# Strassen output projection: product 3 accumulates onto product 5's PSUM bank, with another product order

## Chip, cores and metric

The kernel runs on one core of one Trainium2 chip. The metric is the device time of one execution in microseconds (us); lower is better. The engines named below are TensorE (PE in the profile; its weight loads are PEld), VectorE (DVE), ScalarE (ACT), GpSimd (POOL) and SyncE (SP), whose instruction stream here only issues DMA transfers.

## What is computed

One layer of a decoder trunk. Four head groups (a convolution module, causal pooling, stick-breaking attention, cross-attention into memory) make a mixed activation of 2048 columns for 2048 prompt tokens and for 32 sample tokens; that is projected to 1024 columns, normalised twice and added to the residual. The change touches only the projection and what follows it:

```python
mix = jnp.concatenate([y_c * silu(cg), y_p * silu(pg), y_s * silu(sg), y_m * silu(mg)], axis=-1)
out = rms_norm(mix @ w_out, post_g)      # 2048 x 2048 @ 2048 x 1024
...
y_prompt = rms_norm(x + out, final_g)
```

Everything is float32.

## The kernel before

The product `mix @ w_out` is done by the Strassen-Winograd scheme: tokens are split in two row blocks (even and odd tiles of 128 tokens), the inner dimension in two halves, the output columns in two halves of 512, and seven products of half-size blocks replace eight. The products carry the numbers 1, 7, 2, 6, 4, 5, 3. Product `prod` for token block `i` (0 to 7, each a pair of token tiles 2i and 2i+1) is called (prod, i) here; block 8 (`LAST`, L1545) holds the 32 sample tokens and takes only products 1, 2, 5 and 3.

`order` (L1883 to L1887) lists the products as TensorE runs them; TensorE's order is written by hand, the order on the other engines is made by the program's planner when it is built, from the order in which the code emits the instructions and from estimated durations. `parts` splits each product into two halves h of the inner dimension. The loop at L2051 walks over the parts. For each one `out_part` (L1922) issues the matmuls: 4 chunks of 128 inner rows, each with three matmuls (high times high, high times low, low times high, since each float32 factor is split in a rounded high part and a low remainder), so 24 matmuls of 128x512 for a whole product, all summed in one PSUM bank (`acc`). There are eight banks in rotation by then (`accp`, `accp2`). Ahead of the matmuls, `prepare` (L2035) loads the rows (`out_load`, DMA on SP), adds or subtracts row blocks (`out_combine`, POOL or DVE), rounds to the high part (`out_high`, ACT) and `lows` has DVE make the low part (`out_low`, L1696, tile `ml`), some two products ahead. The right-hand factors are prepared in the same way (`weight_sum`, `weight_high`, `weight_low`, L1586 to L1597).

When a product is complete, `out_ready` (L1702) takes it out. `U2` and `U3` are sums of products 1, 7 and 6, one SBUF tile of 128x512 for each token block.

* Product 4: DVE adds U3 in place in PSUM (L1740), ACT sums its squares (`square`, L1700), DVE multiplies by `post_g` (L1743). This is the left half of token tile 2i+1.
* Product 5: DVE first adds the product to U2 (L1739), then adds U3 to the product in place in PSUM (L1740); squares and the multiplication follow. This is the right half of tile 2i+1, which is now whole, and `out_tile` ends it.
* Product 3: DVE adds U2 (which by now contains product 5) in place; squares and multiplication follow. This is the right half of tile 2i, and `out_tile` ends that one. Its left half, `c11`, was put to DRAM earlier; `out_first` (L1752) fetches it into one of two buffers (`oh`) and `out_factor` (L1758, POOL) multiplies it by `post_g`.

`out_tile` (L1761) loads the residual rows `xt` (tile `oxt`), turns the sums of squares into a factor (L1769 on DVE, L1770 on ACT, L1771 on DVE), adds the residual half by half (L1775, DVE), sums squares again (L1776, ACT), makes the second factor (L1779, L1780, L1781), scales the tile (L1786, DVE) and stores it (L1788). The closing part of tile 15 is put off and emitted within that of tile 14, the last tile of the program.

Of the kernel before, what the change touches and what calls it, by code (L numbers as in the profile page):

```python
# [13 lines left out]
ALU = mybir.AluOpType  # L14
# [73 lines left out]
def kernel(  # L88
# [9 lines left out]
    pe, act, dve, pool, sp = nc.tensor, nc.scalar, nc.vector, nc.gpsimd, nc.sync  # L98
# [1446 lines left out]
    LAST = 8  # L1545
# [152 lines left out]
    def square(c, t, half):  # L1698
        rows = P if t < 16 else NS
        act.activation(out=junk[:rows], in_=c[:rows], func=AF.Square, accum_out=ssk[:rows, t, half : half + 1])  # L1700

    def out_ready(prod, i, o):  # L1702

        if i == LAST:
            if prod == 5:
                return
            both = (ope.tile([P, 512], F32, tag="oh", name="both3", bufs=OH) if prod == 3 else
                    op.tile([P, 512], F32, name=f"both{prod}", bufs=1))
            act.copy(both[:NS], o[NS : 2 * NS])
            dve.tensor_tensor(out=both[:NS], in0=both[:NS], in1=o[:NS], op=ALU.add)  # L1710
            if prod == 1:
                keep["s"] = both
            elif prod == 2:
                dve.tensor_tensor(out=both[:NS], in0=both[:NS], in1=keep["s"][:NS], op=ALU.add)
                square(both, 16, 0)
                keep[16, 0] = both
            else:
                dve.tensor_tensor(out=o[:NS], in0=both[:NS], in1=keep["s"][:NS], op=ALU.add)
                square(o, 16, 1)
                dve.tensor_tensor(out=o[:NS], in0=o[:NS], in1=gpost[:NS, 512:], op=ALU.mult)  # L1720
                dve.tensor_tensor(out=keep[16, 0][:NS], in0=keep[16, 0][:NS], in1=gpost[:NS, :512], op=ALU.mult)
                out_tile(16, keep[16, 0], o)
            return
        t = 2 * i + (prod in (4, 5))
        if prod == 1:
            act.copy(U2[:, i], o)
        elif prod == 7:
            dve.tensor_tensor(out=U3[:, i], in0=o, in1=U2[:, i], op=ALU.add)
        elif prod == 6:
            dve.tensor_tensor(out=U3[:, i], in0=o, in1=U3[:, i], op=ALU.add)  # L1730
            dve.tensor_tensor(out=U2[:, i], in0=o, in1=U2[:, i], op=ALU.add)
        elif prod == 2:
            c = opw.tile([P, 512], F32, tag="c11", name=f"c11_{i}", bufs=1)
            dve.tensor_tensor(out=c, in0=o, in1=U2[:, i], op=ALU.add)
            square(c, t, 0)
            sp.dma_start(c11d[i], c)
        else:
            if prod == 5:
                dve.tensor_tensor(out=U2[:, i], in0=o, in1=U2[:, i], op=ALU.add)  # L1739
            dve.tensor_tensor(out=o, in0=o, in1=(U2 if prod == 3 else U3)[:, i], op=ALU.add)  # L1740
            half = 0 if prod == 4 else 1
            square(o, t, half)
            dve.tensor_tensor(out=o, in0=o, in1=gpost[:, 512 * half : 512 * half + 512], op=ALU.mult)  # L1743
            keep[t, half] = o
            if prod != 4:
                out_tile(t, keep[t, 0], keep[t, 1])
            if (prod, i) == (3, 0):
                out_first(2)
            if prod == 5 and i != 2 or (prod, i) == (3, 1):
                out_factor(2 if prod == 3 else i)  # L1750
# [10 lines left out]
    def out_tile(t, a, b):  # L1761

        rows = P if t < 16 else NS
        xt = ope.tile([P, D], F32, tag="oxt", name=f"oxt{t}", bufs=OX)[:rows]
        sp.dma_start(xt, xp[P * t : P * t + P, :] if t < 16 else xs)
        if t != 14:
            keep["ss"] = ope.tile([P, 6], F32, tag="oss", name=f"oss{t}", bufs=1)
        ss = keep["ss"][:rows, 3:] if t == 14 else keep["ss"][:rows]
        dve.tensor_tensor(out=ss[:, 0:1], in0=ssk[:rows, t, 0:1], in1=ssk[:rows, t, 1:2], op=ALU.add)  # L1769
        act.activation(out=ss[:, 0:1], in_=ss[:, 0:1], func=AF.Sqrt, bias=eps_t[:rows], scale=1.0 / D)  # L1770
        dve.reciprocal(out=ss[:, 0:1], in_=ss[:, 0:1])  # L1771
        last = t == 14
        halves = (slice(0, 512), slice(512, 1024))
        for n, (hs, src) in enumerate(zip(halves, (a[:rows], b[:rows]))):
            dve.scalar_tensor_tensor(out=xt[:, hs], in0=src, scalar=ss[:, 0:1], in1=xt[:, hs], op0=ALU.mult, op1=ALU.add)  # L1775
            act.activation(out=junk[:rows], in_=xt[:, hs], func=AF.Square, accum_out=ss[:, n + 1 : n + 2])  # L1776
        if last:
            keep.pop("end")()
        dve.tensor_tensor(out=ss[:, 1:2], in0=ss[:, 1:2], in1=ss[:, 2:3], op=ALU.add)  # L1779
        act.activation(out=ss[:, 1:2], in_=ss[:, 1:2], func=AF.Sqrt, bias=eps_t[:rows], scale=1.0 / D)  # L1780
        dve.reciprocal(out=ss[:, 1:2], in_=ss[:, 1:2])  # L1781
        dst = y_prompt[0, P * t : P * t + P, :] if t < 16 else y_sample.rearrange("b t d -> (b t) d")

        def end():
            for n, hs in enumerate(halves if last else (slice(0, 1024),)):
                dve.scalar_tensor_tensor(out=xt[:, hs], in0=xt[:, hs], scalar=ss[:, 1:2], in1=gfin[:rows, hs],  # L1786
                                         op0=ALU.mult, op1=ALU.mult)
                (wq if n else sp).dma_start(dst[:, hs], xt[:, hs])  # L1788

        if t == 15:  # L1790
            keep["end"] = end
        else:
            end()
# [90 lines left out]
    order += [(p, i) for i in range(2, 6) for p in (2, 6)] + [(2, 6), (2, 7), (2, 8), (6, 6), (6, 7)]  # L1884
    last_ = len(order)
    order += [(4, 0), (4, 1), (5, 0), (5, 1), (4, 2), (5, 2), (3, 0), (3, 1), (3, 2), (5, 8), (3, 8)]
    order += [(p, i) for i in range(3, 8) for p in (4, 5, 3)]  # L1887
    parts = [(p, i, h) for p, i in order for h in range(2)]
    last_ *= 2
    lead_ = parts[: 2 * LEAD]  # L1890
    raws, mix, accs, keep, stores = {}, {}, {}, {}, []
# [30 lines left out]
    def out_part(x):  # L1922

        prod, i, h = x
        rows = P if i < LAST else 2 * NS
        cont = i == LAST and prod == 3
        bank = 5 if cont else prod, i
        if bank not in accs:
            p_ = accp if accp2 is None or len(accs) % 8 < 3 else accp2
            accs[bank] = p_.tile([P, 512], F32, tag="acc", name=f"acc{prod}_{i}", bufs=3 if p_ is accp else 5)  # L1930
        o, m = accs[bank], mix.pop(x)
        for k in range(4):

            ms = ((0, 0), (0, 1), (1, 0)) if i < LAST else ((0, 0), (0, 1))
            for n, (a, w) in enumerate(ms):
                pe.matmul(o[:rows], lhsT=m[a][:, k, :rows], rhs=W[prod, 4 * h + k][w],  # L1936
                          start=not cont and h == k == n == 0,
                          stop=h == 1 and k == 3 and n == len(ms) - 1 and (prod != 5 or i < LAST))
            yield
        if h:  # L1940
            done.append((prod, i, o))
# [109 lines left out]
    for n, x in enumerate(parts):  # L2051
        if n == last_:
            ow.close()
            x6.close()
            ope = oy.enter_context(tc.tile_pool(name="ope", bufs=1, side="right", reuse_waits="tile"))
            gpost = ope.tile([P, D], F32, name="gpost", bufs=1)
            gfin = ope.tile([P, D], F32, name="gfin", bufs=1)
            sp.dma_start(gpost, post_g[0].partition_broadcast(P))
            sp.dma_start(gfin, final_g.partition_broadcast(P))
        prod, i, h = x  # L2060
        if prod == 4 and not h and i != 2:
            out_first(i)
        while (prod, 4 * h + 3) not in W:
            weights_step(wait)
        lows(n + 1)
        for k, p_ in enumerate(out_part(x) if n >= len(lead_) else lead if not n else ()):
            conv_due += 1.0
            while conv_due >= (OPACE if ("conv", 0) in flags else OPACE0):
                conv_due -= OPACE if ("conv", 0) in flags else OPACE0
                next(conv, None)  # L2070
            weights_step(n + k % 4 / 4)
            if not n:

                k, at_ = p_ % 4, p_ // 4
            else:
                at_ = n
            if k % 4 == LOWK:
                lows(at_ - 1 + AHEAD)
            if not n and k == 3:
                prepare(at_ + AHEAD)  # L2080
        while done:
            out_ready(*done.pop(0))
        prepare(max(n, len(lead_) - 1) + AHEAD)
# [32 lines left out]
```

## Time and profile before

| what | value |
|---|---|
| time, median of 3 runs (lowest to highest) | 2400.12 us (2396.64 to 2403.89) |
| the profiled execution: its time | 2409.2 us |
| the profiled execution: span from first to last instruction | 2407.5 us |
| ACT busy in the whole span | 1116.7 us (46%) |
| POOL busy in the whole span | 1291.0 us (54%) |
| products 4, 5 and 3 on TensorE | from 2239.70 to 2390.62 us |
| last DVE instruction ends | 2404.18 us |

Times within the trace count from the start of the span. A row of the timeline gives start, duration, engine, line, operation, tiles (out<-in), shape and how many like it follow one another; in brackets stands how long the engine sat idle before it, and what it waited for. A row of the stages view gives the stretch, its length, then for each of PE, PEld, DVE, ACT and POOL the busy time and the number of instructions, then the granted TensorE clock (1.00 is full speed), the share of the DMA engines and GB/s. Matmuls are pipelined, so one row's duration overlaps the next; on TensorE the distance between starts is what counts. On DVE too a following instruction starts a little before the one ahead of it is through: two adds shown with 0.68 us each start 0.60 us apart.

### The profile page before, as it was taken

To read this page: it belongs to the slowest core of one execution; us is meant where nothing else is said; L and a number is where in the kernel's file an instruction comes from. 1 tells how busy PE (TensorE), PEld (TensorE's weight loads), DVE (VectorE), ACT (ScalarE), POOL (GpSimd) and SP (SyncE) were. 2 spreads that over 40 slices of the span, in tenths; PEclk is the share of its full clock that TensorE was granted. 3 is DMA by queue.
4 is the path that set the end of the run, shared out by engine and by line. 5 is a ranking of instruction groups with operands and counts; after the bars stand their busy time and mean duration, and the time that the engine had idled before them with its cause. 6 is when DMAs were issued, how large, how long until landed. Compare 5 with 4: busy or idle time off the path is not lost. (4 is left out here: it accounts for less than half of the span.)

```text
span 2407.5 us, 42122 instructions
## 1 busy us (share of the span) xinstructions
PE 2285.4 (95%) x15962; PEld 1772.8 (74%) x15962; DVE 1728.3 (72%) x2420; ACT 1116.7 (46%) x1939; POOL 1291.0 (54%) x1323
## 2 busy tenths in 40 slices
PE   8999999999999999999999998899999998989897
PEld 7898888888888777777777776455555566778775
DVE  5332785959747664577877778879898846687898
ACT  5322343242442322223241435788999955443454
POOL 3554545556474555545556553667776854544431
PEclk9999999999999999999999999999999999999998
DMA  6678988878779899877877767834333127887764
GB/s 210 194 257 283 349 295 301 306 259 275 260 253 316 291 351 319 305 268 275 279 265 277 257 214 185 240 77 113 82 92 82 59 71 246 272 276 239 247 230 170
DMA packets 340437, 562.14 MB, mean 233 GB/s; under 512 B 28481, under 2 KB 212929, under 8 KB 323834
## 3 DMA queue, kind: packets, MB, share of 16 engines
q1 hardware_dynamic: 284858, 290.72, 39.2%
q0 software_dynamic: 55376, 268.72, 31.4%
q8 instruction: 126, 2.06, 0.3%
q14 instruction: 77, 0.63, 0.1%
HBM read 469.28 MB, written 90.68 MB: 233 GB/s over the span
## 5 line engine op out<-in xcount | busy, mean ns | idle before, releaser
L974 DVE STREAM_TRANSPOSE T<-kt 128x1024 f32<-128x1024 f32 x256 | 308.5, 1225 | 192.6 <-PE sSA L987 177.6
L941 POOL DMA_INDIRECT vt<-in_cache_v_dram,idv x256 | 252.8, 988 | 251.3 <-PE sO L1026 190.4
L629 DVE SCALAR_TENSOR_TENSOR cacc<-U,par,cacc 128x512 f32<-128x512 f32 x480 | 360.2, 750 | 11.5
L1327 POOL TENSOR_TENSOR be<-be,E 128x512 f32<-128x512 f32 (+2 forms) x320 | 303.5, 956 | 116.9 <-DVE E L1318 46.7
L1318 DVE TENSOR_TENSOR_SCAN E<-gam,cr,ZM 128x513 f32<-128x513 f32 x192 | 233.0, 1265 | 14.6 <-ACT gam L1303 13.4
L941 POOL DMA_INDIRECT kt<-in_cache_k_dram,idk x128 | 127.2, 994 | 203.0 <-DVE T L974 164.3
L1338 PEld LDWEIGHTS AT<-ident,be 128*128 128x128 f32 x1088 | 117.4, 142 | 126.3 <-ACT at L1344 45.1
L1936 PE MATMUL acc<-wohi,mh 128*128 128x512 f32 (+1 forms) x480 | 194.2, 405 | 1.8 <-DVE mh L1696 1.4
L1303 ACT ACTIVATE gam<-S,nbias_bc 128x1024 f32<-128x1024 f32 (+1 forms) x160 | 172.4, 1077 | 50.1 <-issue 19.6
L1936 PE MATMUL acc<-wolo,mh 128*128 128x512 f32 (+1 forms) x480 | 190.8, 398 | 0.0
L1936 PE MATMUL acc<-wohi,ml 128*128 128x512 f32 x448 | 179.4, 400 | 11.4 <-DVE ml L1696 11.2
L1298 PE MATMUL S<-kT,Q 128*128 128x512 f32 (+1 forms) x640 | 177.0, 400 | 7.9 <-ACT be L1305 2.6
L1305 ACT ACTIVATE be<-S,bias_bc 128x1024 f32<-128x1024 f32 (+1 forms) x160 | 171.3, 1071 | 0.0
L1338 PE MATMUL AT<-ident,be 128*128 128x128 f32 x1088 | 157.5, 283 | 13.4 <-DVE at L1342 4.1
L1354 PE MATMUL av<-at,V 128*64 128x512 f32 (+3 forms) x640 | 152.9, 556 | 1.7 <-DVE sbo L1359 1.7
L987 PE MATMUL sSA<-T,W 128*32 128x128 f32 x4096 | 140.3, 276 | 4.5 <-DVE T L974 2.7
L987 PEld LDWEIGHTS sSA<-T,W 128*32 128x32 f32 x4096 | 104.8, 109 | 42.6 <-issue 34.9
L1696 DVE TENSOR_TENSOR ml<-mr,mh 128x512 fp32r<-128x512 f32 x108 | 101.2, 942 | 39.0 <-ACT mh L1685 38.8
L1298 PEld LDWEIGHTS S<-kT,Q 128*128 128x128 f32 x640 | 106.6, 194 | 24.0 <-ACT be L1305 6.4
L1026 PE MATMUL sO<-vt,saT 128*32 128x512 f32 x1024 | 122.4, 592 | 0.0
L1315 DVE TENSOR_TENSOR_SCAN E<-gam,ZM 128x128 f32<-128x128 f32 (+3 forms) x128 | 96.3, 804 | 30.4 <-ACT gam L1303 23.6
L1344 ACT COPY at<-AT 128x512 f32<-128x512 f32 x192 | 108.9, 656 | 14.4 <-PE AT L1338 14.4
(573 smaller groups left out, 6034.0 us busy)
## 6 DMA issues: line engine op xcount, KB each, us to landing
Q<-qd SPq DMA_DIRECT2D x64, 256.0 KB
mr<-mixd SPq DMA_DIRECT2D x32, 512.0 KB
mr<-mixd SPq DMA_DIRECT2D x48, 256.0 KB
wor<-in_w_out_dram SPq DMA_DIRECT2D x20, 512.0 KB
xtp<-in_x_prompt_dram SPq DMA_DIRECT2D x16, 512.0 KB
kT<-kd SPq DMA_DIRECT2D x64, 128.0 KB
wor<-in_w_out_dram SPq DMA_DIRECT2D x32, 256.0 KB
msd<-mr SPq DMA_DIRECT2D x32, 256.0 KB
```

What stands on the lines that cost most here:

```text
L629: dve.scalar_tensor_tensor(out=ps, in0=U[:, a + k : a + k + H], scalar=wd[:, k : k + 1], in1=ps, op0=ALU.mult, op1=ALU.add)
L941: pool.indirect_dma_start(out=dst, out_offset=None, in_=rows, in_offset=bass.IndirectOffsetOnAxis(ap=idx, axis=0))
L974: S["turn"] = dve.transpose(T[:, 2 * hh : 2 * hh + 2].rearrange("p s j t -> p (s j t)"), kt[:, 2 * hh : 2 * hh + 2].rearrange("p s j d -> ...
L987: pe.matmul(sSs[n][32 * g : 32 * g + 32, P * ml : P * (ml + 1)], lhsT=W[:, jj, :], rhs=T[:, :, jj, :], start=i == 0, stop=i == 3, tile_pos ...
L1298: pe.matmul(S[:, j, :w], lhsT=Q[hh][:, x, P * (q2 + j) : P * (q2 + j + 1)], rhs=KT[hp, hh, kc][:, :w], start=x == 0, stop=x == 1)
L1303: act.activation(out=ga[:, :, 512 - w : 512], in_=S[:, :, :w], func=AF.Sigmoid, bias=nbias_bc[:, h : h + 1], scale=-1.0)
L1305: act.activation(out=be[:, :, :w], in_=S[:, :, :w], func=AF.Sigmoid, bias=bias_bc[:, h : h + 1])
L1318: dve.tensor_tensor_scan(out=E[:, j][:, ::-1], data0=ga[:, j][:, ::-1], data1=ZM[:, 0:1].to_broadcast([P, 513]), initial=carry[hh, q2][:, ...
L1327: pool.tensor_tensor(out=be[:, j, :m], in0=be[:, j, :m], in1=E[:, j, 513 - w : 513 - w + m], op=ALU.mult)
L1338: pe.transpose(ap_[:, P * qt : P * (qt + 1)], A[hp, qb, kc, hh, qt][:, P * r : P * (r + 1)], ident)
L1354: pe.matmul(av[64 * hh : 64 * hh + 64, c], lhsT=V[:, 4 * kc + r, 64 * hh : 64 * hh + 64], rhs=ats.pop((hp, qb, kc, r, hh))[:, c], start=dg ...
L1936: pe.matmul(o[:rows], lhsT=m[a][:, k, :rows], rhs=W[prod, 4 * h + k][w], start=not cont and h == k == n == 0, stop=h == 1 and k == 3 and n ...
```

## The change

```diff
         else:
-            if prod == 5:
-                dve.tensor_tensor(out=U2[:, i], in0=o, in1=U2[:, i], op=ALU.add)
-            dve.tensor_tensor(out=o, in0=o, in1=(U2 if prod == 3 else U3)[:, i], op=ALU.add)
             half = 0 if prod == 4 else 1
-            square(o, t, half)
-            dve.tensor_tensor(out=o, in0=o, in1=gpost[:, 512 * half : 512 * half + 512], op=ALU.mult)
-            keep[t, half] = o
+            c = U3[:, i] if prod == 5 else o
+            dve.tensor_tensor(out=c, in0=o, in1=(U2 if prod == 3 else U3)[:, i], op=ALU.add)
+            square(c, t, half)
+            dve.tensor_tensor(out=c, in0=c, in1=gpost[:, 512 * half : 512 * half + 512], op=ALU.mult)
+            keep[t, half] = c
...
-        if t != 14:
+        if not last:
...
     order += [(4, 0), (4, 1), (5, 0), (5, 1), (4, 2), (5, 2), (3, 0), (3, 1), (3, 2), (5, 8), (3, 8)]
-    order += [(p, i) for i in range(3, 8) for p in (4, 5, 3)]
+    order += [(p, i if p > 3 else i - 1) for i in range(3, 7) for p in (4, 5, 3) if p > 3 or i > 3]
+    order += [(4, 7), (3, 6), (5, 7), (3, 7)]
...
-        cont = i == LAST and prod == 3
+        cont = prod == 3
         bank = 5 if cont else prod, i
...
           start=not cont and h == k == n == 0,
-          stop=h == 1 and k == 3 and n == len(ms) - 1 and (prod != 5 or i < LAST))
+          stop=h == 1 and k == 3 and n == len(ms) - 1 and (prod != 5 or i < LAST),
+          skip_group_check=cont and i < LAST)
...
-        if prod == 4 and not h and i != 2:
+        if prod == (4 if i < 2 else 5) and not h and i not in (2, LAST):
             out_first(i)
```

Product 3 of every token block now starts on the bank that still holds product 5 and adds onto it, as block 8 did already. So the add of product 5 to U2 is gone, and the right half of tile 2i+1 may no longer be made in that bank: it is written to U3's slice in SBUF, and the squares, the multiplication by `post_g` and the residual add read it there. From block 3 on, product 3 comes one token block later: (4,3), (5,3), (4,4), (5,4), (3,3), (4,5), (5,5), (3,4), (4,6), (5,6), (3,5), (4,7), (3,6), (5,7), (3,7). For these blocks the fetch of `c11` is issued at the start of product 5, not of product 4. The lines with `last` only move a name. `skip_group_check` concerns a check at build time.

More of the change, by code (lines that the diff above doesn't have):

```diff
@@ L1763, in out_tile @@
         rows = P if t < 16 else NS
+        last = t == 14
         xt = ope.tile([P, D], F32, tag="oxt", name=f"oxt{t}", bufs=OX)[:rows]
         sp.dma_start(xt, xp[P * t : P * t + P, :] if t < 16 else xs)
-        if t != 14:
+        if not last:
             keep["ss"] = ope.tile([P, 6], F32, tag="oss", name=f"oss{t}", bufs=1)
-        ss = keep["ss"][:rows, 3:] if t == 14 else keep["ss"][:rows]
+        ss = keep["ss"][:rows, 3:] if last else keep["ss"][:rows]
         dve.tensor_tensor(out=ss[:, 0:1], in0=ssk[:rows, t, 0:1], in1=ssk[:rows, t, 1:2], op=ALU.add)
@@ L1771, in out_tile @@
         dve.reciprocal(out=ss[:, 0:1], in_=ss[:, 0:1])
-        last = t == 14
         halves = (slice(0, 512), slice(512, 1024))
```

## The prediction

> **What bounds the kernel now.** I read the page's busy times first, then the stretch in which products 4, 5 and 3 run, stage by stage.
>
> ```profile
> PE 2285.4 (95%) x15962; PEld 1772.8 (74%) x15962; DVE 1728.3 (72%) x2420; ACT 1116.7 (46%) x1939; POOL 1291.0 (54%) x1323
> ```
>
> ```profile
> 2270.00:2297.00 27.00, 26.56 (x114) 19.90 (x112) 24.84 (x43) 11.51 (x33) 5.10 (x3) 1.00 0.69 239
> 2297.00:2320.00 23.00, 18.95 (x71) 13.32 (x72) 20.61 (x35) 12.71 (x34) 12.24 (x8) 0.93 0.70 247
> 2320.00:2385.00 65.00, 64.88 (x283) 52.80 (x283) 60.73 (x110) 34.08 (x94) 12.84 (x9) 1.00 0.59 206
> 2385.00:2404.30 19.30, 5.61 (x25) 4.16 (x23) 14.04 (x30) 7.94 (x24) 0.00 (x0) 0.74 0.28 109
> ```
>
> TensorE bounds nearly the whole kernel, and the change leaves its matmuls as they are. It can only gain where TensorE is not full: in the 23 us from 2297 on and after the last matmul. From 2320 to 2385 TensorE is full (283 matmuls in 65 us, 0.23 us each, so 5.5 us for a product of 24 and 16.5 us for a round of products 4, 5 and 3) while DVE is at 93%: it keeps up without slack.
>
> TensorE's own rows in the second stretch, and its stage view around the largest gap:
>
> ```profile
> 2297.31 0.44 PE L1936 MATMUL acc<-wohi,mh 128*64 128x512 f32 x1 [0.39 <-DVE mh L1696]
> 2300.44 0.44 PE L1936 MATMUL acc<-wohi,mh 128*64 128x512 f32 x1 [1.06 <-DVE mh L1696]
> 2306.43 0.50 PE L1936 MATMUL acc<-wohi,ml 128*128 128x512 f32 x1 [0.75 <-DVE ml L1696]
> 2314.47 0.50 PE L1936 MATMUL acc<-wohi,ml 128*128 128x512 f32 x1 [1.93 <-DVE ml L1696]
> ```
>
> ```profile
> 2312.40:2315.80 3.40, 1.47 (x7) 1.11 (x7) 3.40 (x8) 0.81 (x2) 1.91 (x1) 1.00 0.60 200
> 2315.80:2319.20 3.40, 3.40 (x10) 2.63 (x9) 3.40 (x5) 3.04 (x9) 3.15 (x3) 0.50 0.93 272
> ```
>
> In (3,8), (4,3) and (5,3) TensorE waits 4.13 us in all for low parts that DVE makes late. Behind the longest wait the granted clock is 0.50 for 3.4 us, which costs half of that, 1.7 us. So 5.8 us are there to be had.
>
> The end, on TensorE and on DVE:
>
> ```profile
> 2384.62 0.39 PE L1936 MATMUL acc<-wohi,ml 128*128 128x512 f32 x1
> 2384.85 0.39 PE L1936 MATMUL acc<-wohi,mh 128*128 128x512 f32 x1
> ...
> 2390.22 0.40 PE L1936 MATMUL acc<-wohi,ml 128*128 128x512 f32 x1
> ```
>
> ```profile
> 2380.05 0.69 DVE L1740 TENSOR_TENSOR acc<-acc,U 128x512 f32<-128x512 f32 x1
> ...
> 2384.39 0.69 DVE L1740 TENSOR_TENSOR acc<-acc,U 128x512 f32<-128x512 f32 x1
> ...
> 2389.77 1.28 DVE L1786 SCALAR_TENSOR_TENSOR oxt<-oxt,oss,gfin 128x1024 f32<-128x1024 f32 x1
> 2390.97 0.68 DVE L1739 TENSOR_TENSOR U<-acc,U 128x512 f32<-128x512 f32 x1
> 2391.57 0.69 DVE L1740 TENSOR_TENSOR acc<-acc,U 128x512 f32<-128x512 f32 x1
> ...
> 2394.39 1.41 DVE L1775 SCALAR_TENSOR_TENSOR oxt<-acc,oss,oxt 128x512 f32<-128x512 f32 x2
> 2395.72 0.69 DVE L1740 TENSOR_TENSOR acc<-acc,U 128x512 f32<-128x512 f32 x1
> ...
> 2399.70 0.75 DVE L1775 SCALAR_TENSOR_TENSOR oxt<-oh,oss,oxt 128x512 f32<-128x512 f32 x1
> ...
> 2402.76 1.42 DVE L1786 SCALAR_TENSOR_TENSOR oxt<-oxt,oss,gfin 128x512 f32<-128x512 f32 x2
> ```
>
> The last matmul of (5,7) starts at 2384.62 and is through at 2385.01; the add that the change keeps (L1740) comes at 2391.57. I call this distance the lag of a product: 6.56 us here. Product (3,7) is done at 2390.62, its add comes at 2395.72 (lag 5.1), and the last scaling ends at 2404.18. From the end of (5,7) to that end are 19.17 us. In them DVE is a late reader, and TensorE never waits for it. The adds at 2380.05 and 2384.39 are those of (3,6) and (4,7).
>
> **The change part by part.** *The eight removed adds.* Their row (L1739), those of the other DVE operations that read a bank, and that of the low parts, which read SBUF alone (duration in ns: least/median/most):
>
> ```profile
> L1775 DVE SCALAR_TENSOR_TENSOR oxt<-acc,oss,oxt x25: 729/743/752, 2276.0 to 2400.4; 128x512 f32<-128x512 f32 x24, 32x512 f32<-32x512 f32 x1
> L1743 DVE TENSOR_TENSOR acc<-acc,gpost x24: 671/699/700, 2269.9 to 2397.5; 128x512 f32<-128x512 f32 x24
> L1740 DVE TENSOR_TENSOR acc<-acc,U x22: 668/686/694, 2264.4 to 2395.7; 128x512 f32<-128x512 f32 x22
> L1739 DVE TENSOR_TENSOR U<-acc,U x8: 672/680/685, 2263.8 to 2391.0; 128x512 f32<-128x512 f32 x8
> ```
>
> ```profile
> L1696 DVE TENSOR_TENSOR ml<-mr,mh x40: 658/684/1776, 2261.8 to 2385.1; 128x512 fp32r<-128x512 f32 x40
> ```
>
> Each add takes 0.60 us of DVE's queue (2390.97 to 2391.57). The adds of (5,0) and (5,1) free nothing:
>
> ```profile
> 2263.82 0.68 DVE L1739 TENSOR_TENSOR U<-acc,U 128x512 f32<-128x512 f32 x1
> ...
> 2268.12 0.67 DVE L1739 TENSOR_TENSOR U<-acc,U 128x512 f32<-128x512 f32 x1
> 2269.87 1.90 DVE L1743 TENSOR_TENSOR acc<-acc,gpost 128x512 f32<-128x512 f32 x3 [1.08 <-DMA gpost<-in_post_g_dram]
> ```
>
> Both stand ahead of a wait for the load of `post_g`, which ends at 2269.87 whatever DVE did before. Without that cover they would be worth 1.2 us. The add of (5,2) stands ahead of the four gaps, so they shrink by 0.60 in all. A gap at 2314 that is shorter may also leave the clock up: I take half of the 1.7, 0.85. The stage gains 1.45; its bounds are 0 (the planner fills the place with other work) and 5.8 (no gap at all).
>
> *The half kept in SBUF.* Eight multiplications and eight residual adds get a second SBUF input. The four bank-fed rows above are flat (0.75 us at most), while L1696 with two SBUF inputs reaches 1.78. [...] For the price I use rows: POOL runs 9 operations in 65 us, 2.3 a round; each can hold up DVE by 1.78 - 0.68 = 1.1 us; two further operations of 0.7 in a round of 16.5 raise the chance of a hit by 0.09; 2.3 x 0.09 x 1.1 = 0.2 us a round. Bounds: 0, and 0.7 (two hits of the 1.1 in three rounds). ACT's squares lie beside DVE work either way.
>
> *Product 3 a block later.* Its first matmul must wait for the add of (5,i), the bank's last reader. Two or three other products lie between for every block but the last, 11 us at least, against the lags of 4.9 to 6.6 us worked out here: nothing. The fetch of `c11` is issued 5.5 us later and may wait on SP for its buffer, and POOL's multiplication for it. Behind these stand row loads and the next sum of rows, needed some five parts (14 us) on; I cost this at nothing, and at up to 1 us if that cover is gone. Fewer banks are taken, and none is waited for now.
>
> *The end: a new wait.* Between (5,7) and (3,7) nothing lies any more. TensorE stands until DVE has run the add of (5,7); behind it stand the 24 last matmuls, and the last tile waits for these. What it costs hangs on the lag L of (5,7). One way: now 6.56, less 0.60 for its own removed add and for those of blocks 3 to 6, is 3.56. Another: (5,7) began 24 matmuls ahead of 2384.85, so (4,7) ended at about 2379.5 and lags 4.9 now (2384.39); less 2.4 is 2.5; keep that for (3,6). From the add of one right half to the next DVE takes 4.15 us (2391.57 to 2395.72), plus up to two low parts of (3,7), 1.2, against 5.5 on TensorE: 2.4 at most. With the 0.2 a round given back I take L = 3.0, bounds 0.1 and 6.6.
>
> ```profile
> 2313.74 0.67 DVE L1696 TENSOR_TENSOR ml<-mr,mh 128x512 fp32r<-128x512 f32 x1
> ```
>
> From its end (2314.41) to the released matmul (2314.47) are 0.06 us, my estimate for a hand-over. A stand of 3.75 us is longer than the one that brought the half clock at 2315.80, so I expect it again within (3,7), partly under the wait: 1.2 (bounds 0 and 3.4, two such stretches). [...]
>
> After (3,7) DVE no longer lags, since tile 15 fits into the 5.8 us of (3,7). From add to residual add is 2.82 us for tile 15 (2391.57 to 2394.39) and 3.98 for tile 14 now, with the close of tile 15 in between: 3.4. Then 4.48 to the end (2399.70 to 2404.18): 7.9.
>
> L 3.0 + add 0.69 + 0.06 + matmuls 5.77 (2384.85 to 2390.62) + clock 1.2 + 0.06 + 7.9 = 18.7, against 19.17: -0.5. With -1.45 the sum is -1.9 us. The profiled execution took 2409.2 (span 2407.5), 9.1 above the median of the runs shown; it goes to 2407.3, and the median from 2400.1 to 2398.2.
>
> **The rivals.** *A, slower:* the add of (5,7) falls behind the whole closing of tile 12, as its first add does today (2390.97, right behind L1786 at 2389.77). From an add to the end of its tile are 8.5 us (2395.72 to 2404.18), so L is 2.5 + 8.5 - 5.5 = 5.5, and with the two low parts and a lag of 4 it is 8.2. At 7 with 2.5 for the clock the tail is 24.0, +4.8, and nothing gained before: 2404.9. It decides from L plus clock above 4.7. Against it: today's next add, at 2395.72, does pass the closing of tile 15.
>
> *B, much faster:* freed from 0.60 a round, DVE never makes TensorE wait before the end (-5.8), and L falls to 1.2 with 0.6 for the clock (tail 16.3, -2.9): 2391.4. For it: every gap ends on DVE. Against it: only one removed add stands before them.
>
> [...]
>
> **How the numbers follow.** Forecast 0.45 (2398.2, itself 2394 to 2402), B 0.25, C 0.17, A 0.13. A measurement here tells about 0.3% (7.2 us) from no change. Faster than 2392.9: most of B and a little of the forecast, 0.25. Slower than 2407.3: a third of A, and a planner's order worse than I can read, 0.11. Within: 0.64. The range runs from 2389.5 (B with its bounds) to 2406 (A).
>
> **What would show it.** Right: 8 L1739 gone; one new gap of 2 to 5 us on TensorE in front of its last 24 matmuls, ended by DVE's add, and a half clock behind it; gaps before 2320 smaller by about 0.6 to 1.5; L1743 and L1775 rows from U with maxima above 1 us. Wrong: no gap ahead of (3,7), or one above 6 us; new gaps between 2320 and 2385; the gaps in (3,8) to (5,3) gone or grown.

## The result, and the profile after

The changed kernel takes 2405.66 us (median, 2397.59 to 2411.53), the kernel before on the same chip 2399.93 us (2393.84 to 2403.89): a ratio of 1.0023, 95% interval 1.0013 to 1.0033. It is slower by 5.7 us, where 1.9 us faster was forecast. The time lies within the predicted range, and the difference is below the 0.3% (7.2 us) that I took a measurement to need; the interval is about 0.1% to either side, so it does tell the change from none, and the sign is the other one. The nearest case is rival A (2404.9), in part by luck: A puts its whole loss of 4.8 us behind (5,7), where 2.8 us are found below.

The page of the changed kernel, and the stages view of its profiled execution (2406.4 us; columns as in the prediction) from the start of (4,0) to the end of (5,7), and from there to the end of the last scaling:

```profile
PE 2283.3 (95%) x15962; PEld 1772.4 (74%) x15962; DVE 1725.2 (72%) x2412; ACT 1116.7 (46%) x1939; POOL 1288.3 (54%) x1323
```

```profile
2236.21:2379.38 143.17, 136.14 (x585) 106.93 (x583) 126.75 (x211) 73.74 (x191) 41.59 (x27) 1.00 0.68 233
2379.38:2401.34 21.96, 7.67 (x24) 5.80 (x24) 14.55 (x30) 8.20 (x24) 0.00 (x0) 0.75 0.25 97
```

VectorE has eight instructions fewer, as intended (2412 for 2420). The last stretch is 21.94 us (2379.38 to 2401.32), where the kernel before had 19.17 and I forecast 18.7. The timeline of TensorE around it, (5,7)'s last matmul and then (3,7)'s first and last:

```profile
2378.99 0.39 PE L1936 MATMUL acc<-wohi,ml 128*128 128x512 f32 x1
2386.23 0.76 PE L1936 MATMUL acc<-wohi,mh 128*128 128x512 f32 x1 [6.86 <-DVE U L1740]
...
2393.51 0.40 PE L1936 MATMUL acc<-wohi,ml 128*128 128x512 f32 x1
```

TensorE stands for 7.0 us (7.24 between the starts, less 0.23 for a matmul), ended by the add of (5,7), and then runs (3,7) from 2386.23 to 2393.91: 7.68 us where before it took 5.77. The stages view in pieces of 3.41 us shows why; the clock is the third figure from the right:

```profile
2380.04:2383.45 3.41, 0.00 (x0) 0.00 (x0) 2.73 (x7) 1.13 (x4) 0.00 (x0) 1.00 0.38 156
2383.45:2386.87 3.42, 0.64 (x2) 0.57 (x3) 2.12 (x5) 2.28 (x7) 0.00 (x0) 0.50 0.45 153
2386.87:2390.28 3.41, 3.41 (x10) 2.64 (x9) 2.65 (x6) 1.23 (x5) 0.00 (x0) 0.50 0.40 159
2390.28:2393.69 3.41, 3.41 (x16) 2.59 (x14) 1.61 (x3) 0.84 (x3) 0.00 (x0) 1.00 0.00 0
```

An empty piece is followed by two at half clock. (3,7) begins at the end of the first (2 matmuls) and runs through the second: 10 matmuls in it, 16 in the next piece at full clock.

What VectorE did in the meantime (timeline, from the add of (3,6) to the first operations behind the add of (5,7), and the last chain):

```profile
2379.60 0.69 DVE L1740 TENSOR_TENSOR acc<-acc,U 128x512 f32<-128x512 f32 x1
...
2381.10 0.70 DVE L1742 TENSOR_TENSOR acc<-acc,gpost 128x512 f32<-128x512 f32 x1 [0.23 <-ACT junk L1700]
...
2382.22 0.16 DVE L1771 RECIPROCAL oss<-oss 128x1 f32<-128x1 f32 x1 [0.36 <-ACT oss L1770]
2382.47 0.75 DVE L1774 SCALAR_TENSOR_TENSOR oxt<-oh,oss,oxt 128x512 f32<-128x512 f32 x1
2383.14 0.74 DVE L1774 SCALAR_TENSOR_TENSOR oxt<-acc,oss,oxt 128x512 f32<-128x512 f32 x1
2384.82 0.16 DVE L1778 TENSOR_TENSOR oss<-oss 128x1 f32<-128x1 f32 x1 [0.93 <-ACT junk L1775]
2385.34 0.16 DVE L1780 RECIPROCAL oss<-oss 128x1 f32<-128x1 f32 x1 [0.36 <-ACT oss L1779]
2385.42 0.67 DVE L1740 TENSOR_TENSOR U<-acc,U 128x512 f32<-128x512 f32 x1
2386.01 1.28 DVE L1785 SCALAR_TENSOR_TENSOR oxt<-oxt,oss,gfin 128x1024 f32<-128x1024 f32 x1
...
2393.95 0.70 DVE L1740 TENSOR_TENSOR acc<-acc,U 128x512 f32<-128x512 f32 x1 [1.08 <-PE acc L1936]
...
2399.90 1.42 DVE L1785 SCALAR_TENSOR_TENSOR oxt<-oxt,oss,gfin 128x512 f32<-128x512 f32 x2
```

(5,7) is through at 2379.38 and its add starts at 2385.42, a lag of 6.04 us. In these VectorE stands idle four times, 0.23 + 0.36 + 0.93 + 0.36 = 1.88 us, each time for ScalarE, while the add that TensorE waits for is due. The other 4.16 us are work that stands ahead of it in the fixed order: the add and the multiplication of (3,6), the last low part, the end of a scaling, and the close of tile 12. The add's place is behind the close of tile 12 up to L1780, and that close goes to and fro between VectorE and ScalarE. So the tail is 6.04 of lag, 0.81 from the add's start to the released matmul, 7.68 for (3,7), and 7.41 to the end (2393.91 to 2401.32).

The profiled execution of one kernel below, block7_apart_again, was disturbed (3166.65 us at a mean clock of 0.654), so its trace isn't read.

### The profile page after: what moved, and what is told of

Its sections match the earlier page's. It is cut to its first block, busy times and chain, and to the rows that moved or that the text cites. A ratio compares the mean times of both kernels' runs of the same rounds, so it can differ in the third digit from the quotient of the medians.

```text
span 2404.7 us, 42119 instructions
## 1 busy us (share of the span) xinstructions
PE 2283.3 (95%) x15962; PEld 1772.4 (74%) x15962; DVE 1725.2 (72%) x2412; ACT 1116.7 (46%) x1939; POOL 1288.3 (54%) x1323
## 5 line engine op out<-in xcount | busy, mean ns | idle before, releaser
L1936 PE MATMUL acc<-wohi,ml 128*128 128x512 f32 x448 | 179.3, 400 | 12.6 <-DVE ml L1696 12.6
L1696 DVE TENSOR_TENSOR ml<-mr,mh 128x512 fp32r<-128x512 f32 x108 | 94.5, 881 | 39.3 <-ACT mh L1685 38.9
```

## The experiments

Each kernel was timed beside the kernel before; the two kernels of the change are in the table too. A ratio is that to the runs of the kernel before beside it, whose medians lay between 2399.32 and 2400.68, so the medians of two rows don't compare to a microsecond. "Wait" is TensorE's in front of (3,7), "tail" the time from the end of (5,7) to the last scaling, "from (4,3)" that from the first matmul of (4,3), where the orders of products part, to the last scaling; all three are from the profiled execution.

| kernel | median us | ratio to before (95%) | wait us | tail us | from (4,3) us |
|---|---|---|---|---|---|
| before | 2399.93 | | 0 | 19.17 | 101.83 |
| before, second time | 2398.03 | 0.9997 (0.9987 to 1.0008) | 0 | 19.01 | 101.12 |
| the change | 2405.66 | 1.0023 (1.0013 to 1.0033) | 7.01 | 21.94 | 105.59 |
| the change, second time | 2405.35 | 1.0022 (1.0012 to 1.0033) | 7.03 | 22.32 | 105.97 |
| wait_only | 2402.65 | 1.0008 (0.9998 to 1.0018) | 6.98 | 22.45 | 105.16 |
| wait_only_again | 2403.59 | 1.0017 (1.0003 to 1.0030) | 7.04 | 22.11 | 104.39 |
| block7_apart | 2403.15 | 1.0010 (1.0000 to 1.0020) | 0 | 20.51 | 104.60 |
| block7_apart_again | 2402.65 | 1.0016 (1.0002 to 1.0030) | not read | not read | not read |
| order_alone | 2399.52 | 1.0004 (0.9992 to 1.0016) | 0 | 18.67 | 102.24 |
| add_first | 2402.88 | 1.0011 (0.9999 to 1.0023) | 3.90 | 19.37 | 103.69 |
| dummy_add | 2401.47 | 1.0011 (0.9999 to 1.0024) | 5.82 | 20.72 | 102.37 |
| end_swapped | 2397.74 | 0.9993 (0.9980 to 1.0005) | 1.30 | 24.49 with (3,6) | 103.02 |
| end_swapped_again | 2401.55 | 1.0010 (1.0000 to 1.0020) | 1.31 | 24.49 with (3,6) | 105.29 |
| swapped_apart | 2401.70 | 1.0006 (0.9995 to 1.0017) | 0 | 25.05 with (3,6) | 103.31 |

**Both kernels a second time.** before_again and after_again are copies, for the spread of the traces.

> The kernel before once more, for a second profile of its last stage. In the first one the stage from the first matmul of (4,0) to the end of the last scaling took 164.5 us with 4.1 us of waits in (3,8) to (5,3) and a half clock of 3.4 us behind them. If these waits and the half clock are usual, the stage takes 163 to 166 us again. If that execution had more of them than is usual, it takes 158 to 162 us, and the slowdown measured for the change (5.7 us) fits the wait at the end better than the two first profiles do (0.6 us).

> The changed kernel once more. Theory 1 (the new wait at the end is what costs): TensorE stands 6 to 7.5 us in front of the 24 matmuls of (3,7), the clock is halved behind it, and from the end of (5,7) to the last scaling are 21 to 23 us. Theory 2 (the later place of product 3 costs ahead of the end): the waits of TensorE from (4,3) to (4,7) come to 5 us or more again, against 4 in the kernel before.

The tails repeat within 0.4 us. Ahead of them they don't: from the start of (4,0) to the end of (5,7) the kernel before takes 145.31 and 142.04 us, the changed one 143.17 and 143.07. One pair of traces would have shown a gain of 2.1 us there, the other a loss of 1.0. Of the 3.3 us between the two traces of the kernel before, 2.7 lie ahead of (4,3): from (4,0) to there the first took 62.65 us and the second 59.93, and all others that were read 59.40 to 60.27. The whole stage, up to the last scaling, took 161.05 us in before_again, so the 164.5 of the first trace were more than is usual. What TensorE waited for low parts, grouped by line (count, busy us, mean ns, idle us before them), for before, before_again, the change and after_again in turn; the windows begin with (4,0) and end at 2391, 2365, 2386 and 2387 us, and between these ends and that of (5,7) no low part is waited for:

```profile
L1936 PE MATMUL acc<-wohi,ml 128*128 128x512 f32 x193 | 77.0, 399 | 5.8 <-DVE ml L1696 5.6
```

```profile
L1936 PE MATMUL acc<-wohi,ml 128*128 128x512 f32 x177 | 70.1, 396 | 5.8 <-DVE ml L1696 5.8
```

```profile
L1936 PE MATMUL acc<-wohi,ml 128*128 128x512 f32 x185 | 73.2, 396 | 7.0 <-DVE ml L1696 7.0
```

```profile
L1936 PE MATMUL acc<-wohi,ml 128*128 128x512 f32 x185 | 73.8, 399 | 5.3 <-DVE ml L1696 5.2
```

5.6 and 5.8 before, 7.0 and 5.2 after: the gain that I forecast there isn't to be found.

**The wait alone, and the change without it.** wait_only is the kernel before, in its order, with the shared bank for block 7 only:

```diff
-            if prod == 5:
+            if prod == 5 and i < 7:
...
+            c = U3[:, i] if (prod, i) == (5, 7) else o
...
-        cont = i == LAST and prod == 3
+        cont = i >= 7 and prod == 3
```

> The kernel before, in its old product order, but products 5 and 3 of block 7 alone share a bank as in the change. Theory 1 (the wait at the end): a wait of 6 to 7.5 us ahead of (3,7), half clock behind it, 21 to 23 us from the end of (5,7) to the last scaling, and 2 to 5 us slower than the kernel before. Theory 2 (the places of the other blocks): within 1.5 us of the kernel before.

block7_apart is the change with a bank each for products 5 and 3 of block 7, so that nothing waits ahead of (3,7):

```diff
-            c = U3[:, i] if prod == 5 else o
+            if prod == 5 and i == 7:
+                dve.tensor_tensor(out=U2[:, i], in0=o, in1=U2[:, i], op=ALU.add)
+            c = U3[:, i] if prod == 5 and i != 7 else o
...
-        cont = prod == 3
+        cont = prod == 3 and i != 7
```

> The change, but products 5 and 3 of block 7 alone as they were before: an add of product 5 to U2, and a bank of its own for (3,7). So the last 24 matmuls need not wait; everything ahead of them stays as in the change. Theory 1: no wait ahead of (3,7), full clock there, the end 1.5 to 6 us earlier than in the changed kernel; if the wait is the whole slowdown, it equals the kernel before within 2 us. Theory 2: it stays 4 us or more above the kernel before.

Both were run a second time, to see how the 5.7 us divide:

> The same kernel as the one in which only block 7 shares a bank, in the order of before. Open is whether the wait ahead of (3,7) is the whole 5.7 us of the change or a half of it. From the traces the stretch from the end of (5,7) to the last scaling is 22.45 us with the wait and 19.0 to 19.2 without, so I expect 3.3 us, a ratio of 1.0014. If the wait were all of it, the ratio would be 1.0022 or more; the first result was 1.0008, and the two together decide.

> The change without the wait: only block 7 keeps a bank for each product. If the wait is all of the change's cost, this lies at 1.0000 of the kernel before (0.9993 to 1.0005). If about 2.5 us lie elsewhere (in the order, the shared banks of the blocks before, or the half clock behind the wait within (4,3)), it lies at 1.0010 again, as the first time.

In the old order and with seven of the eight adds in place, the wait is there at once, of the same length, and so is the lag of (5,7): 5.99 us (2374.26 to 2380.25) and 6.05 in the second trace, where the change has 6.04 and 6.05. The ratios are 1.0008 and 1.0017 for the wait without the rest, 1.0010 and 1.0016 for the rest without the wait: about 3 us each (0.0012 and 0.0013 of 2400), and together they make the 5.7. All four intervals reach from about nothing to twice that, so the division is rough. For the wait the tails say the same: 22.45 and 22.11 against 19.17 and 19.01 are 3.2 us.

**The order alone.** The kernel before with the change's order of products and its later fetch of `c11`, each product in a bank of its own and all adds kept:

```diff
-    order += [(p, i) for i in range(3, 8) for p in (4, 5, 3)]
+    order += [(p, i if p > 3 else i - 1) for i in range(3, 7) for p in (4, 5, 3) if p > 3 or i > 3]
+    order += [(4, 7), (3, 6), (5, 7), (3, 7)]
...
-        if prod == 4 and not h and i != 2:
+        if prod == (4 if i < 2 else 5) and not h and i not in (2, LAST):
```

> The kernel before with the new product order and the later fetch of c11 alone: product 3 in banks of its own, the adds to U2 kept. Theory 1: no wait ahead of (3,7); within 3 us of the kernel before. Theory 2: 4 us or more above the kernel before, with more or longer waits of TensorE from (4,3) to (4,7).

1.0004: the order by itself costs nothing that shows in the time (the interval reaches to 1.0016), and its tail is the shortest, 18.67 us. Its VectorE at the end, and after it that of block7_apart, which runs the same operations for block 7:

```profile
2378.43 0.68 DVE L1739 TENSOR_TENSOR U<-acc,U 128x512 f32<-128x512 f32 x1
2379.44 0.16 DVE L1779 TENSOR_TENSOR oss<-oss 128x1 f32<-128x1 f32 x1 [0.34 <-ACT junk L1776]
2379.52 0.69 DVE L1740 TENSOR_TENSOR acc<-acc,U 128x512 f32<-128x512 f32 x1
```

```profile
2383.27 0.16 DVE L1780 TENSOR_TENSOR oss<-oss 128x1 f32<-128x1 f32 x1 [0.93 <-ACT junk L1777]
...
2383.87 0.67 DVE L1740 TENSOR_TENSOR U<-acc,U 128x512 f32<-128x512 f32 x1
2384.46 1.27 DVE L1787 SCALAR_TENSOR_TENSOR oxt<-oxt,oss,gfin 128x1024 f32<-128x1024 f32 x1
2385.65 0.69 DVE L1742 TENSOR_TENSOR acc<-acc,U 128x512 f32<-128x512 f32 x1
```

In order_alone the planner puts the first add of (5,7) into the time in which the close of tile 12 waits for ScalarE's squares, and the second follows early: 5.59 us after the end of (5,7) at 2373.93. In block7_apart VectorE idles 0.93 there, the first add comes behind the close and the second behind the scaling too: 7.89 after 2377.76. In the kernel before the two stand side by side and the second is at 6.56. The tails follow these places: 18.67, 20.51 and 19.17 us, less 5.59, 7.89 and 6.56 leave 13.1, 12.6 and 12.6. Where the planner puts an add among the steps of a close makes 1.3 us here (7.89 against 6.56), without any wait of TensorE.

**The add of (5,7) moved up.** The change, with the close of tile 12 from its residual add on kept back and emitted behind the add of (5,7):

```diff
+            add = dve.tensor_tensor(out=c, in0=o, in1=(U2 if prod == 3 else U3)[:, i], op=ALU.add)
+            if (prod, i) == (5, 7):
+                with tc.issue_after(add.ins):
+                    keep.pop("rest")()
...
+        if t == 12:
+            keep["rest"] = lambda: out_close(t, a, b, xt, ss, rows, last, halves)
```

> The changed kernel with one order forced on VectorE: the closing of tile 12 (from its residual add on) stands behind the add of (5,7). If the lag of that add is the work that the fixed order puts ahead of it, the wait ahead of (3,7) falls from 7.0 us to 3 to 4.5 us and the kernel gets 1 to 3 us faster than the change. If VectorE is merely behind by its load, the wait stays at 6 us or more and nothing is gained.

```profile
2381.42 0.67 DVE L1740 TENSOR_TENSOR U<-acc,U 128x512 f32<-128x512 f32 x1
2382.01 0.74 DVE L1784 SCALAR_TENSOR_TENSOR oxt<-oh,oss,oxt 128x512 f32<-128x512 f32 x1
```

```profile
2378.11 0.39 PE L1946 MATMUL acc<-wohi,ml 128*128 128x512 f32 x1
2382.24 0.76 PE L1946 MATMUL acc<-wohi,mh 128*128 128x512 f32 x1 [3.74 <-DVE U L1740]
```

The first fence is VectorE's timeline, the second TensorE's. With the add ahead of the residual adds the lag is 2.92 (from 2378.50), the wait 3.90, and the tail 19.37, level with before. That the lag meets the 3.0 that I had forecast is chance, since I had it from less work and not from another place. TensorE's wait follows the add's place. The ratio is 1.0011; its interval overlaps that of the change, so the gain rests on the trace, and nothing shows it to be better than the kernel before.

**Five adds put back.** The change with an add after each of (5,3) to (5,7) whose result nobody reads:

```diff
+            if prod == 5 and i > 2:
+                dve.tensor_tensor(out=U2[:, i - 3], in0=o, in1=U2[:, i], op=ALU.add)
```

> The changed kernel with the removed adds put back for blocks 3 to 7 as adds whose result nobody reads. If the lag is a chain of waits between VectorE and ScalarE in a fixed order, the five adds go into idle time: lag of (5,7) 5.5 to 7 us as in the change, time within 2 us of the change. If it is VectorE's load, the lag grows by 0.6 us a round to 8 us or more, and the time by 3 us.

1.0011, so 3.0 us more work for VectorE don't make the change slower; the point value is even lower, though its interval overlaps the change's. I had expected the lag of the change, 5.5 to 7 us. It is shorter, because the planner made another order of it: two rows of VectorE, behind the add without a reader, and the matmul that was released:

```profile
2377.02 0.68 DVE L1740 TENSOR_TENSOR U<-acc,U 128x512 f32<-128x512 f32 x1
2378.04 0.16 DVE L1780 TENSOR_TENSOR oss<-oss 128x1 f32<-128x1 f32 x1 [0.33 <-ACT junk L1777]
2378.11 0.68 DVE L1742 TENSOR_TENSOR U<-acc,U 128x512 f32<-128x512 f32 x1
```

```profile
2378.95 0.76 PE L1938 MATMUL acc<-wohi,mh 128*128 128x512 f32 x1 [5.66 <-DVE oss L1782]
```

The useless add (2377.02) fills idle time ahead of L1780, and the real one (2378.11) comes ahead of the second factor's reciprocal, lag 4.82 (from 2373.29). The trace names L1782 as releaser, but that is the operation next in line; what the matmul needs is the add that ends at 2378.79.

**Another end.** The change with (5,7) ahead of (3,6), so that a product lies between (5,7) and (3,7), and with the close of tile 12 kept back in place of that of tile 15:

```diff
-        if t == 15:
+        if t == 12:
...
-    order += [(4, 7), (3, 6), (5, 7), (3, 7)]
+    order += [(4, 7), (5, 7), (3, 6), (3, 7)]
```

> The change with another end: (4,7), (5,7), (3,6), (3,7), so that one product lies between (5,7) and (3,7); the close of tile 12 is put off into tile 14 in place of that of tile 15. Theory 1: with a lag of 6 us against 5.5 us of matmuls the wait ahead of (3,7) is 0 to 2.5 us, and the kernel is 2 to 6 us faster than the change. Theory 2: no more than 1.5 us faster.

> The same kernel as the one that ends in (4,7), (5,7), (3,6), (3,7). My theory (the wait ahead of (3,7) and the half clock behind it are what the change costs; the rest of it gains nothing) expects 0.9980 to 1.0005 of the kernel before again, and at least 4 us less than the changed kernel's 1.0022; it has no reason for a gain over the kernel before. If the removed adds do gain something of their own once the wait is gone, both results lie below 0.9995. If the first result was chance, this one comes out at 1.001 or above.

The first result, 0.9993, looked like a version as good as the kernel before or better; the second is 1.0010. Between them lies no difference to before that can be told. The point values of both are below the change's, though the second interval overlaps. The lag of (5,7) is still 5.92 us in both, and of the wait's 7.0 us 5.7 have gone, because (3,6) runs meanwhile. With a bank each for block 7 on top:

> The same order, but products 5 and 3 of block 7 keep a bank each, so no gap at all ahead of (3,7) (1.3 us in the kernel with the shared bank) and one more add on VectorE. If the remaining 1.3 us wait counts, this is about 1 us (0.05%) faster than the shared one, a difference below what five rounds resolve; in the trace the 1.3 us are gone and the stage from the start of (4,0) to the last scaling is 161 to 162.5 us. Rival: the added add delays the end as much as the wait did, and the stage is as long as that of the shared one, 162.4 us or longer.

No wait is left, and it makes 1.0006, between the two. From the start of (4,0) to the last scaling it takes 162.73 us, end_swapped 162.43 and 164.79: neither side of that expectation is borne out. No version ran that was shown to beat the kernel before.

## Why the prediction was wrong

**The step that failed: "I take L = 3.0".** The wait's place and its releaser were right (one new gap, in front of the last 24 matmuls, ended by the add of (5,7)), the lag wasn't: 6.04 us, near the end of its bounds (6.6), and with it a gap above 6 us, which the prediction had named as a sign of being wrong. Of the 3.0 us taken off the 6.56 for five adds, only the first 0.60 came, that of (5,7)'s own add; the four adds of blocks 3 to 6 brought nothing. The add of (3,6), for which I kept a lag of 2.5, lags 5.7 (2379.60, after the end at 2373.91). There is no backlog that 0.60 us a round works off: wait_only keeps these four adds and has the same lag (5.99). The two lags show it as a sum, too: with 6.04 and the 1.9 of the clock, the prediction's sum gives a tail of 22.4, and 21.94 was measured. The waits of VectorE from the start of (4,3) to the end of (5,7), first before_again, then the change (us in all, times, longest):

```profile
DVE acc L1743 <- ACT junk L1700: 2.2, 5, 0.6
...
DVE ml L1696 <- ACT mh L1685: 0.7, 1, 0.7
```

```profile
DVE acc L1742 <- ACT junk L1700: 3.9, 8, 0.6
DVE ml L1696 <- ACT mh L1685: 1.9, 4, 0.7
```

And the stages view of the same stretch, in the same order:

```profile
2288.27:2370.40 82.13, 78.56 (x338) 62.66 (x337) 76.83 (x135) 43.09 (x118) 21.74 (x14) 1.00 0.60 211
```

```profile
2295.73:2379.40 83.67, 78.65 (x337) 62.36 (x335) 74.84 (x128) 43.10 (x117) 20.97 (x13) 1.00 0.60 206
```

VectorE works 2.0 us less (76.83 to 74.84) and stands 3.5 us more (82.13 - 76.83 = 5.30 to 83.67 - 74.84 = 8.83). The second trace of the change (74.85 of 83.67) and the first of the kernel before (77.03 of 82.68) say the same. Not all of this idle time is that of the adds: order_alone, which keeps them all, already stands 7.47 us in this stretch (76.12 of 83.59), so about two thirds of the 3.5 us come with the order of products, and only the rest with the adds. The order of VectorE's instructions is fixed when the program is built, and a tile's close needs ScalarE at four places, so less work need not pull the later operations forward. I had read "DVE is at 93%" as a queue that is always full; it is a chain with ScalarE in it. That the lag is made by the close's length stood in rival A, and A's "whole closing of tile 12" is what happened, but for the scaling at L1785, which comes behind the add. My argument against A, that an add "does pass the closing of tile 15", didn't carry over to another tile. add_first shows that the place, not the load, decides: L is 2.92 as soon as the add stands ahead of the residual adds.

**The half clock**: it came within (3,7) as forecast, and cost 1.9 for 1.2 (7.68 for 5.77). The wait filled a whole piece of 3.41 us (no matmul from 2380.04 to 2383.45), the following one held 0.64 us of matmuls, and two pieces ran at 0.50.

**The chain after (3,7)**: right, 7.41 for 7.9, and 13.56 before. Here the deferral of tile 15's close paid: with 7.0 us of TensorE standing, VectorE was done with tile 15 and waited for (3,7) itself (1.08 at 2393.95). The wait and the clock make 7.0 + 1.9 = 8.9 us, of which 6.15 (13.56 - 7.41) come back here; the rest is what the tail has grown by, 21.94 - 19.17 = 2.8.

**"The stage gains 1.45"**: not seen. The waits in (3,8) to (5,3) are in fact shorter, 2.15 and 2.27 us in the two traces of the change against 4.13 and 2.94 before, but two others have come, which the prediction named as a sign of being wrong (the second of them in after_again too, with 1.02; the kernel before has one of 0.62 in one trace of two):

```profile
2325.08 0.50 PE L1936 MATMUL acc<-wohi,ml 128*128 128x512 f32 x1 [1.52 <-DVE ml L1696]
2365.75 0.50 PE L1936 MATMUL acc<-wohi,ml 128*128 128x512 f32 x1 [1.26 <-DVE ml L1696]
```

order_alone keeps all adds and has no wait in (3,8) and 2.73 us in (4,3) and (5,3), so the shorter waits aren't the adds' either. dummy_add with the work put back isn't slower. The term was the freed VectorE time again.

**Half in SBUF (rival C)**: the price of 0.2 us a round was my estimate, and no run shows it; nor does one show the 0.25 us that C put on each of the sixteen new operations with two SBUF inputs. The view of the tile `U` in the change (ns, least/median/most):

```profile
L1742 DVE TENSOR_TENSOR U<-U,gpost x8: 677/689/694, 2264.6 to 2387.2; 128x512 f32<-128x512 f32 x8
L1774 DVE SCALAR_TENSOR_TENSOR oxt<-U,oss,oxt x8: 729/741/744, 2269.8 to 2389.2; 128x512 f32<-128x512 f32 x8
```

None of the sixteen took more than 0.69 and 0.74 us, though I had expected maxima above 1 us. Others that had two SBUF inputs already did take longer than their medians in the change (1.28 and 0.68 us), such as a scaling and a low part around (4,3), with 2.02 and 1.75, in whose window POOL works 2.39 us of 3.41. The low parts above 1 us in the kernel before ran beside an operation of POOL as well (1.78 at 2304.60, POOL's from 2303.56 for 2.26), but so did others of 0.67 (2316.93, POOL's from 2316.91 for 1.84). The two rows of the change:

```profile
2294.76 2.02 DVE L1785 SCALAR_TENSOR_TENSOR oxt<-oxt,oss,gfin 128x1024 f32<-128x1024 f32 x1
2296.70 1.75 DVE L1696 TENSOR_TENSOR ml<-mr,mh 128x512 fp32r<-128x512 f32 x1
```

**Rival B** fell with the same step as the forecast: less work on VectorE did not make its results earlier.

**What stays open.** Of the 7.6 us between the forecast (-1.9) and the result (+5.7) the tail makes 3.3 (21.94 for 18.7) and the missing gain 1.45. About 3 us of the 5.7 aren't the wait: block7_apart has none and is at 1.0010 and 1.0016. Its tail is 1.3 to 1.5 us longer than that of before, as late as its second add of (5,7) is later. The traces also show where most of the rest can lie. From (4,3) to the end of (5,7), with the same 336 matmuls, the four traces in the old order take 82.11 to 82.70 us, the two of the change 83.65 each, block7_apart 84.09, add_first 84.33, and order_alone already 83.57, of which its shorter tail makes up a part. So some 1.2 us seem to come with the new order, and with the tail the two traces of the change are 4.3 us longer than those before, from (4,3) on. This is read from one trace of most kernels and no experiment isolates it; dummy_add, in the same order of products with another on VectorE, takes 81.65. The long waits in (4,3), 2.3 to 2.9 us in all kernels that share banks in block 3, are in end_swapped too, which isn't shown to be slower than before, so they don't explain it alone. What the shared banks of the other blocks cost, without the order, wasn't run.

## What to carry to other kernels

Before a saved instruction is counted as time, see whether its engine is late because of its load or because of the chain that it shares with another engine: the idle time between its instructions, with who ended it, tells the two apart (here 1.88 us in four waits for ScalarE, within a lag of 6.04). Where a consumer is to reuse a producer's buffer, look up the place of the last reader in its engine's fixed order: here TensorE waited 7.01 us with the add behind most of the close of tile 12, 3.90 with it ahead of the residual adds (add_first), and 1.30 with another product in between (end_swapped). And where two executions of one kernel differ by 3 us within a stage, as 145.31 and 142.04 do here, two traces settle nothing about 1 us there; the same stage has to be read twice, and cut where the two kernels part.

## What was not expected of the hardware

The half clock comes in pieces of 3.41 us. In the change's clock record every stretch between two changes of the clock is a whole multiple of 3.413 us long (3.41, 6.83 or 10.24 us at half clock); it sets in at 2229.85 and 2383.45, 153.60 us apart, which is 45 times 3.413. The wait in (4,3) falls in the first piece of the first two fences; the columns are those of the stages view again, the first change, then after_again, then wait_only ahead of its gap:

```profile
2294.71:2298.12 3.41, 1.64 (x8) 0.78 (x5) 3.38 (x3) 0.43 (x1) 2.39 (x2) 1.00 0.78 285
2298.12:2301.54 3.42, 3.04 (x13) 2.51 (x14) 3.08 (x7) 2.20 (x6) 0.00 (x0) 1.00 0.81 249
```

```profile
2296.90:2300.32 3.42, 1.15 (x6) 0.63 (x5) 3.42 (x4) 0.31 (x2) 2.16 (x2) 1.00 0.70 269
2300.32:2303.73 3.41, 3.41 (x10) 2.67 (x9) 2.55 (x7) 2.59 (x7) 0.54 (x1) 0.50 0.52 168
```

```profile
2372.68:2376.09 3.41, 1.58 (x7) 0.96 (x6) 3.32 (x7) 0.36 (x2) 0.00 (x0) 1.00 0.38 154
2376.09:2379.50 3.41, 0.00 (x0) 0.00 (x0) 1.89 (x5) 2.25 (x7) 0.00 (x0) 1.00 0.41 151
2379.50:2382.92 3.42, 1.84 (x4) 1.49 (x5) 2.21 (x5) 1.02 (x3) 0.00 (x0) 0.50 0.38 158
2382.92:2386.33 3.41, 3.41 (x9) 2.63 (x8) 2.04 (x6) 1.74 (x5) 0.00 (x0) 0.50 0.00 0
```

The wait is 2.32 us in the one and 2.43 in the other execution of the same code. Where it left 1.64 us of matmuls in its piece, the next ran at full clock; where the pieces cut it otherwise and 1.15 were left, the next ran at half and lost half of its 3.41, 1.7 us. 1.58 (46%; wait_only, 2372.68) was followed by full clock too, and 1.47 (43%) by half in the piece that the prediction shows; a piece that ran at half clock already was followed by another with 1.84 (wait_only, 2379.50). No bound can be read from this: earlier in the change 1.94 was followed by half clock, too:

```profile
2048.95:2052.37 3.42, 1.94 (x12) 1.45 (x11) 3.42 (x8) 3.42 (x10) 1.41 (x2) 1.00 0.87 293
2052.37:2055.78 3.41, 3.41 (x12) 2.83 (x12) 3.00 (x5) 0.89 (x2) 2.58 (x4) 0.50 1.00 349
```

In these two executions a wait of 2.3 to 2.4 us cost 1.7 us of matmuls more or nothing, by where the pieces cut it. It needn't lengthen the stage: both executions take 83.65 us from (4,3) to the end of (5,7), and the one that kept its clock waited 1.52 us for a low part at 2325.08, where the other didn't wait.
